# Second block: convolution taps summed in a PSUM bank, inverse roots partly in PSUM, each head's tail moved into the next head's recurrence

## The chip, the cores and the metric

The kernel is one program on one core of a Trainium2 chip. The core has five engines that matter here: TensorE (PE; its weight loads are listed as PEld), VectorE (DVE), ScalarE (ACT), GpSimd (POOL) and SyncE (SP), which issues DMAs. They share SBUF; TensorE writes into PSUM, eight banks of 512 fp32 columns on 128 partitions, which VectorE and ScalarE read and write too. The metric is the device time of one execution in microseconds, the median over several runs.

## The reference, cut to what matters

The model has two parts, one after the other, on 512 tokens of width 1024: a two-layer block, and a second block. The change lies in the first half of the second block. It computes eight heads of a gated linear recurrence (HGRN2) and a causal depthwise convolution of width 31, both from projections of the same input:

```
z = u @ w_in[l]
zq, zf, zi, zg, zca, zcb, zga, zgb = jnp.split(z, IN_SPLITS, axis=-1)
f = lb + (1.0 - lb) * jax.nn.sigmoid(zf)
o = hgrn2_chunkwise(heads(zq), heads(1.0 - f), heads(zi), heads(jnp.log(f)))
o = rms_norm_2(o, hg_norm_g[l].reshape(HG_HEADS, HG_DV)).reshape(B, S, HG_VW)
y_a = (o * jax.nn.silu(zg)) @ w_a[l]
glu = zca * jax.nn.sigmoid(zcb)
cv = causal_depthwise_conv(glu, conv_w[l], conv_b[l])
cv = jax.nn.silu(layer_norm(cv, conv_ln_g[l], conv_ln_b[l]))
y_b = cv @ w_b[l]
merged = jax.nn.sigmoid(zga) * y_a + jax.nn.sigmoid(zgb) * y_b
h = h + g1 * (merged @ w_out[l])
```

Here `hgrn2_chunkwise` is the recurrence with a decay per feature and step, and each head's output is divided by its root mean square over 128 features (`rms_norm_2`) and multiplied by a gain and by silu(zg). A layer of routed experts (PEER) follows.

## The kernel before, in words

Activations lie feature by feature: 128 features of a block on the partitions, 512 tokens along the free axis. A head of the recurrence is one such block, and so is an eighth of the convolution. Every projection unit (1024 inputs, 128 outputs) is three fp32r products, high by high, high by low and low by high, 24 matmuls of 128x512 on lines 249 to 251. Its weights come by one DMA of 512 KB; ScalarE makes the high half (line 226, `whi`), VectorE or GpSimd the low half (line 227, `wlo`).

`block2` runs a loop over eight heads. For head `hd`, `hgrn_head` is the recurrence, and a background generator is stepped 2.1 times at each of its yields: `conv_block(hd)`, which computes one eighth of the convolution, and then `hgrn_products(hd + 1)`, the four projections of the next head. What the yields set is the order in which the instructions are written down; the framework's planner then orders each engine's queue by its own estimates of when operands are ready, and the engines run these queues in that fixed order, each waiting for its operands.

`hgrn_head` goes through nine doubling levels. On a level GpSimd makes `ke` (lines 1431, 1433), VectorE makes `qe` (1435, 1437), TensorE multiplies them into a bank of the PSUM group "a" (1441 to 1466), VectorE or ScalarE copies the result out (1443 and others), and the running products `suf` (GpSimd, 1471) and `pre` (VectorE, 1472) are updated. Then TensorE forms the output in a bank of group "m", ScalarE copies it to `o` and squares it, TensorE sums the squares over the partitions (line 350), and `rsqrt` (lines 355 to 373) computes the inverse root on VectorE: a start value from the bits (362), and three Newton steps of three instructions (366 to 368), all on tiles of 128x4 in SBUF. The tail of a head follows: `rowbc` broadcasts the root to all partitions with TensorE matmuls (line 380, eight in the trace), VectorE multiplies (1491) and GpSimd multiplies by the gate (1492, `og`).

`conv_block` makes two projections and the gated input `xp`, then 31 taps. The first is ScalarE's (1325), 22 are VectorE's (1340), each adding `xp` shifted and scaled to `a`, a part of the SBUF tile `cv`; 8 are made by ScalarE (1334) and added up in `b` by GpSimd (1338). Line 1343 adds the two sums. After the loop come the projections of the two gates, `layer_stats` and `layer_norm` of the convolution, and the output products.

PSUM is cut into groups of banks by `set_banks`; block 2 runs with four banks in "m" and four in "a".

Of the kernel before, what the change touches and what calls it, by code (L numbers as in the profile page):

```python
# [11 lines left out]
I32 = mybir.dt.int32  # L12
U32 = mybir.dt.uint32
AF = mybir.ActivationFunctionType
ALU = mybir.AluOpType
P = 128
T = 512
NEG = -1.0e38
EPS = 1e-6
# [129 lines left out]
class Ker:  # L149
# [31 lines left out]
        mk = lambda n: [pool.tile([P, 2, 256], F32, tag=f"{n}{l}", name=f"{n}{l}") for l in range(2)]  # L181
        self.kT, self.vM = mk("kT"), mk("vM")

    def set_banks(self, m, a, o=0):

        self.banks.close()
        mk = lambda n, b: self.banks.enter_context(
            self.tc.tile_pool(name=n, bufs=b, space=bass.MemoryType.PSUM, reuse_waits="tile")
        )
        self.ps = {}  # L190
        for k, n in (("o", o), ("m", m), ("a", a)):
            if n:
                self.ps[k] = mk("p" + k, n)

# [157 lines left out]
                start=(b == 0 and t == 0), stop=(b == nb - 1), skip_group_check=True,  # L352
            )

    def rsqrt(self, ps, n, scale, post=1.0):

        nc, sm = self.nc, self.small
        t = lambda s: sm.tile([P, 8], F32, tag="rs_" + s, name=self.nm("rs_" + s))
        v = t("v")
        nc.vector.tensor_scalar(v[:, :n], ps, scale, EPS, ALU.mult, ALU.add)  # L360
        y = t("y")
        nc.vector.tensor_scalar(y[:, :n].bitcast(I32), v[:, :n].bitcast(I32), -0.5, 1597463007.0, ALU.mult, ALU.add)
        for i in range(3):
            last = i == 2
            a, b, y2 = t("a"), t("b"), t("y")
            nc.vector.tensor_tensor(a[:, :n], y[:, :n], y[:, :n], op=ALU.mult)  # L366
            nc.vector.scalar_tensor_tensor(b[:, :n], a[:, :n], -0.5, v[:, :n], ALU.mult, ALU.mult)  # L367
            nc.vector.scalar_tensor_tensor(y2[:, :n], b[:, :n], 1.5, y[:, :n], ALU.add, ALU.mult)
            y = y2
        if post != 1.0:  # L370
            y2 = t("y")
            nc.vector.tensor_scalar(y2[:, :n], y[:, :n], post, None, ALU.mult)
            y = y2
        return y
# [838 lines left out]
class KerC(KerB):  # L1213
# [13 lines left out]
    def block2(self, after, want):  # L1227
        nc, tc = self.nc, self.tc
        u, win = self.h, self.I["win"]
        with tc.tile_pool(name="b2", bufs=1, reuse_waits="tile") as pool:  # L1230
            og = pool.tile([P, 8, T], F32, tag="og", name="og")
            cv = pool.tile([P, 8, T], F32, tag="cv", name="cv")
            csum = pool.tile([P, T], F32, tag="csum", name="csum")
            with tc.tile_pool(name="b2h", bufs=1, reuse_waits="tile") as hp:
                bufs = {"keep": 2, "kq": KQ, "p": CP, "s": SS, "o": 3, "o1": 1, "o2": 1, "suf": 1, "b": 1}

                def f(name, tag):
                    b = bufs.get(tag, 2)
                    return hp.tile([P, T], F32, tag=tag, name=self.nm(name), bufs=b)

                sc = [hp.tile([P, 4, P], F32, tag=f"sc{i}", name=f"sc{i}") for i in range(2)]
                for s in sc:
                    nc.gpsimd.memset(s, 0.0)

                def background(hd, out):
                    yield from self.conv_block(hd, u, f, hp, cv)
                    if hd == 0:
                        nc.scalar.activation(csum, cv[:, 0, :], AF.Copy)
                    else:
                        nc.gpsimd.tensor_tensor(csum, csum, cv[:, hd, :], op=ALU.add)  # L1250
                    if hd < 7:
                        yield from self.hgrn_products(hd + 1, u, f, out)

                ins = {}
                for _ in self.hgrn_products(0, u, f, ins):
                    pass
                for hd in range(8):
                    nxt = {}
                    bg, due = background(hd, nxt), 0.0
                    for _ in self.hgrn_head(hd, f, sc[hd % 2], og, **ins):  # L1260
                        due += NC
                        while due >= 1:
                            due -= 1
                            next(bg, None)
                    for _ in bg:
                        pass
                    ins = nxt
            with tc.tile_pool(name="b2g", bufs=1, reuse_waits="tile") as gp:
                ga = gp.tile([P, 8, T], F32, tag="ga", name="ga")
                gb = gp.tile([P, 8, T], F32, tag="gb", name="gb")  # L1270
                self.gemm([win[48 + i] for i in range(8)], u, lambda i, ps, s: nc.scalar.activation(ga[:, i, :], ps, AF.Sigmoid))
                a = self.act_pair(gp, "oga", tag="p2")
                for k in range(8):
                    self.split(og[:, k, :], a[0][:, k, :], a[1][:, k, :], nc.gpsimd if k % 2 else nc.vector)
                rb = self.layer_stats(cv, csum)
                self.gemm([win[56 + i] for i in range(8)], u, lambda i, ps, s: nc.scalar.activation(gb[:, i, :], ps, AF.Sigmoid))
                b = self.new_h()
                self.layer_norm(cv, rb, b)

                def ev_a(i, ps, s):  # L1280
                    nc.vector.tensor_tensor(ga[:, i, :], ga[:, i, :], ps, op=ALU.mult)

                self.gemm([self.I["wa2"][i] for i in range(8)], a, ev_a)
                m = self.act_pair(gp, "mg", tag="p2")

                turn = {"t": 0, "q": 0, "acc": 0}

                def h2(kind):
                    i = turn[kind] = (turn[kind] + 1) % 8
                    if kind == "acc":  # L1290
                        return csum[:, i % 2 * 256 : i % 2 * 256 + 256]
                    return cv[:, i, :256] if kind == "t" else cv[:, i, 256:]

                self.h2 = h2

                def ev_b(i, ps, s):
                    nc.vector.tensor_tensor(gb[:, i, s], gb[:, i, s], ps[:, s], op=ALU.mult)
                    nc.gpsimd.tensor_tensor(ga[:, i, s], ga[:, i, s], gb[:, i, s], op=ALU.add)
                    self.split(ga[:, i, s], m[0][:, i, s], m[1][:, i, s])

                self.gemm([self.I["wb2"][i] for i in range(8)], b, ev_b, tail=3, mid=lambda hf: iter(()))

                def ev_o(i, ps, s):
                    x = self.xT[:, i, s]
                    nc.vector.scalar_tensor_tensor(x, ps[:, s], self.mod[:, 16 + i : 17 + i], x, ALU.mult, ALU.add)

                self.gemm(
                    [self.I["wo2"][i] for i in range(8)], m, ev_o, head=3, tail=4,
                    mid=lambda hf: after(slice(hf * 256, hf * 256 + 256)), want=want,
                )  # L1310

    def conv_block(self, i, u, f, pool, cv):

        nc = self.nc
# [6 lines left out]
        nc.scalar.activation(s, pss[1], AF.Sigmoid)  # L1321
        nc.vector.tensor_tensor(xp[:, K - 1 :], s, pss[0], op=ALU.mult)
        w = lambda j: self.v("conv2", j * 8 + i)
        a = cv[:, i, :]
        nc.scalar.activation(a, xp[:, 0:T], AF.Identity, scale=w(0), bias=self.v("conv2b", i))  # L1325
        b = None
        nd = ND
# [2 lines left out]
        while on_dve or on_act:  # L1330
            if on_act:
# [3 lines left out]
                if b is None:  # L1335
                    b = p
# [3 lines left out]
                nc.vector.scalar_tensor_tensor(a, xp[:, j : j + T], w(j), a, ALU.mult, ALU.add)  # L1340
            del on_dve[:2]
            yield
        nc.vector.tensor_tensor(a, a, b, op=ALU.add)

    def layer_stats(self, cv, csum):

# [57 lines left out]
        nc.scalar.activation(vt, pt, AF.Copy)  # L1404
        out.update(q=q, k=k, pre=pre, vt=vt, zg=zg)

    def hgrn_head(self, hd, f, scd, og, q, k, pre, vt, zg):

        nc, sm = self.nc, self.small
        C = lambda x, c: x[:, c * P : c * P + P]  # L1410
# [11 lines left out]
        for l in range(9):  # L1422
            m = 1 << l
# [14 lines left out]
            if m <= 16:  # L1438
                ps = self.psum()
# [4 lines left out]
            elif m == 32:  # L1444
                ps = self.psum()
# [7 lines left out]
            elif m == 64:  # L1453
                ps = self.psum()
# [3 lines left out]
            elif m == 128:  # L1458
                ps = self.psum()
# [3 lines left out]
            else:  # L1463
                ps = self.psum()
# [16 lines left out]
        o = f("o", "o")  # L1481
# [2 lines left out]
        nc.scalar.activation(sq, o, AF.Square)  # L1484
        pst = self.psum()
        self.colsum(pst, sq, 0, 1, 4)
        r = self.rsqrt(pst[:, :4], 4, 1.0 / P)
        yield
        rb = self.rowbc(r)
        t = f("t", "o")  # L1490
        nc.vector.scalar_tensor_tensor(t, o, self.v("hgn", hd), rb, ALU.mult, ALU.mult)
        nc.gpsimd.tensor_tensor(og[:, hd, :], t, zg, op=ALU.mult)

# [453 lines left out]
```

## Time and profile before

| | |
|---|---|
| median of 3 runs | 3586.81 us (3584.31 to 3593.23) |
| profiled execution | 3589.47 us |
| its span, first to last instruction | 3587.6 us |
| mean granted TensorE clock | 0.973 |
| busy: PE, DVE, ACT, POOL | 3407.2, 2391.1, 1436.3, 1313.2 us |
| head loop of the second block | about 1590 to 2050 us of the span |

A row of the profile names the line of the kernel, the engine, the operation, output and inputs (`cv<-xp,vec,cv`), shapes and a count, then busy time and the mean duration of one in ns. "Idle before" is the time that the engine stood still just ahead of these instructions, with what ended it. Times within the span are microseconds from its start. PEclk is the TensorE clock that was granted, as a share of full speed.

### The profile page before, as it was taken

How to read it: one execution, taken by the hardware profiler on the slowest of the kernel's cores; microseconds unless marked ns; L12 is line 12 of the kernel's file. 1: busy time of each engine (PE TensorE's matmuls, PEld its weight loads, DVE VectorE, ACT ScalarE, POOL GpSimd, SP SyncE). 2: the span in 40 equal slices, each digit the busy share in tenths (PEclk: the TensorE clock that was granted, in tenths of full speed). 3: DMA queues.
4: the chain of work that ended last, by engine and by line, in shares of the span. 5: the costliest groups of instructions: out<-in, count | busy, mean ns of one | idle time of the engine just before them, and what ended most of it. 6: DMA issues, size and time to landing. Idle time of an engine off the chain costs nothing.

```text
span 3587.6 us, 51001 instructions
## 1 busy us (share of the span) xinstructions
PE 3407.2 (95%) x19199; PEld 3065.0 (85%) x19199; DVE 2391.1 (67%) x4361; ACT 1436.3 (40%) x2496; POOL 1313.2 (37%) x974
## 2 busy tenths in 40 slices
PE   7999989999999999988888899998999999999999
PEld 6888788888777888876767678898999999999999
DVE  6675475445665754469898844589576654988874
ACT  4444432224555322233323332333767653333332
POOL 1322230003332210136656522246776767333310
PEclk9999999999999999998989999999999999999998
DMA  3210144221111532211111122226999898999972
GB/s 124 71 36 30 59 158 159 96 92 60 42 47 36 200 135 95 94 54 54 59 53 54 63 85 83 88 102 211 322 319 319 312 335 294 401 363 362 362 286 77
DMA packets 207350, 555.47 MB, mean 155 GB/s; under 512 B 18048, under 2 KB 85760, under 8 KB 203904
## 3 DMA queue, kind: packets, MB, share of 16 engines
q1 hardware_dynamic: 170240, 417.98, 33.3%
q0 software_dynamic: 36864, 134.23, 10.3%
q8 instruction: 151, 2.47, 0.3%
q14 instruction: 95, 0.78, 0.1%
HBM read 504.43 MB, written 47.71 MB: 154 GB/s over the span
## 4 chain that ended last, share of the span: by engine, by line
PE 54%; DVE 11%; POOL 2%; issue 2%; ACT 1%; DMA 0%; DVEq 0%; POOLq 0%; ACTq 0%
PE psa L1855 15%; PE psm L249 11%; PE psm L251 11%; PE psm L250 11%; DVE cv L1340 3%; PE psa L1800 2%; DVE wlo L227 1%; PE psa L350 1%; PE psa L380 1%; DVE rs_b L367 1%; POOL ke L1431 0%; DVE rs_a L366 0%; POOL suf L1471 0%; DVE eq L1746 0%; PE psa L1671 0%
## 5 line engine op out<-in xcount | busy, mean ns | idle before, releaser
L226 ACT ACTIVATE whi<-raw 128x1024 fp32r<-128x1024 f32 x559 | 590.9, 1059 | 1380.3 <-PE psm L250 763.7
L249 PE MATMUL psm<-hh,whi 128*128 128x512 f32 (+2 forms) x2768 | 1026.1, 371 | 25.9 <-ACT whi L226 14.8
L251 PE MATMUL psm<-hh,wlo 128*128 128x512 f32 (+2 forms) x2768 | 1007.0, 364 | 6.1 <-POOL wlo L227 4.6
L250 PE MATMUL psm<-hl,whi 128*128 128x512 f32 (+2 forms) x2768 | 1005.2, 363 | 1.3 <-DVE hl L1223 1.3
L227 DVE TENSOR_TENSOR wlo<-raw,whi 128x1024 fp32r<-128x1024 f32 x397 | 545.8, 1376 | 227.6 <-ACT whi L226 225.4
L249 PEld LDWEIGHTS psm<-hh,whi 128*128 128x128 f32 x2768 | 533.4, 193 | 81.5 <-ACT whi L226 16.1
L251 PEld LDWEIGHTS psm<-hh,wlo 128*128 128x128 f32 x2768 | 533.6, 193 | 64.4 <-POOL wlo L227 5.6
L250 PEld LDWEIGHTS psm<-hl,whi 128*128 128x128 f32 x2768 | 533.8, 193 | 52.7 <-issue 2.4
L227 POOL TENSOR_TENSOR wlo<-raw,whi 128x1024 fp32r<-128x1024 f32 x162 | 392.2, 2425 | 287.5 <-ACT whi L226 226.1
L1855 PE MATMUL psa<-gah,wlo 128*128 128x384 f32 (+2 forms) x1048 | 350.8, 335 | 0.0
L1855 PE MATMUL psa<-gah,whi 128*128 128x384 f32 (+2 forms) x1048 | 350.7, 335 | 0.0
L1855 PE MATMUL psa<-gal,whi 128*128 128x384 f32 (+2 forms) x1048 | 350.5, 334 | 0.0
L565 POOL TENSOR_TENSOR relu<-relu 128x512 f32<-128x512 f32 (+1 forms) x70 | 80.6, 1153 | 539.9 <-ACT whi L226 406.2
L1594 POOL DMA_INDIRECT rg<-in_vr_dram,rei x128 | 164.7, 1286 | 282.9 <-DVE racc L1613 267.3
L1855 PEld LDWEIGHTS psa<-gah,wlo 128*128 128x128 f32 x1048 | 200.0, 191 | 0.2 <-DVE wlo L227 0.2
L1855 PEld LDWEIGHTS psa<-gah,whi 128*128 128x128 f32 x1048 | 200.0, 191 | 0.0
L1855 PEld LDWEIGHTS psa<-gal,whi 128*128 128x128 f32 x1048 | 200.0, 191 | 0.0
L1605 DVE SCALAR_TENSOR_TENSOR rg<-rg,hT 128x1024 f32<-128x1024 f32 x128 | 153.5, 1213 | 58.5 <-DMA rg<-in_ur_dram,rei 58.4
L1340 DVE SCALAR_TENSOR_TENSOR cv<-xp,vec,cv 128x512 f32<-128x512 f32 x176 | 176.2, 1001 | 9.7 <-ACT cv L1325 7.1
L1613 DVE SCALAR_TENSOR_TENSOR racc<-rg,rw,racc 128x1024 f32<-128x1024 f32 x127 | 162.6, 1281 | 2.1 <-DMA rg<-in_vr_dram,rei 1.7
L1594 POOL DMA_INDIRECT rg<-in_ur_dram,rei x128 | 128.9, 1007 | 79.0 <-DVE rg L1605 59.7
L1772 DVE TENSOR_TENSOR oA<-io,tr 128x512 f32<-128x512 f32 x96 | 66.0, 688 | 129.2 <-PE psa L1800 115.0
(519 smaller groups left out, 6070.7 us busy)
## 6 DMA issues: line engine op xcount, KB each, us to landing
raw<-in_pu_dram SPq DMA_DIRECT2D x128, 512.0 KB, 4.8
raw<-in_pv_dram SPq DMA_DIRECT2D x128, 512.0 KB, 5.7
raw<-in_wup_dram SPq DMA_DIRECT2D x64, 512.0 KB, 3.5
raw<-in_wdn_dram SPq DMA_DIRECT2D x64, 512.0 KB, 3.5
raw<-in_win_dram SPq DMA_DIRECT2D x64, 512.0 KB, 3.4
araw<-in_ada_dram SPq DMA_DIRECT2D x48, 512.0 KB, 4.3
G<-gb SPq DMA_DIRECT2D x24, 1024.0 KB, 6.6
gt<-G SPq DMA_DIRECT2D x64, 384.0 KB, 7.9
```

Of the source, the lines that this page charges most:

```text
L226: nc.scalar.activation(hi, src, AF.Copy)
L227: (eng or nc.vector).tensor_tensor(lo, src, hi.bitcast(F32), op=ALU.subtract)
L249: nc.tensor.matmul(ps, wh[:, k, :], ah[:, kk, s], start=start, stop=False)
L250: nc.tensor.matmul(ps, wh[:, k, :], al[:, kk, s], start=False, stop=False)
L251: nc.tensor.matmul(ps, wl[:, k, :], ah[:, kk, s], start=False, stop=stop)
L565: nc.gpsimd.tensor_tensor(r, r, r, op=ALU.mult)
L1340: nc.vector.scalar_tensor_tensor(a, xp[:, j : j + T], w(j), a, ALU.mult, ALU.add)
L1594: pin(nc.gpsimd.indirect_dma_start(out=g, out_offset=None, in_=self.I["ur" if i < P else "vr"], in_offset=bass.IndirectOffsetOnAxis(ap=ei[ ...
L1605: pin(nc.vector.scalar_tensor_tensor(g, g, 1.0, hT, ALU.mult, ALU.mult, accum_out=dots[:, c : c + 1]))
L1613: pin(nc.vector.scalar_tensor_tensor(acc, g, w[:, c : c + 1], acc, ALU.mult, ALU.add))
L1800: nc.tensor.matmul(pg[:, i * P : i * P + P], A[:, i, :], B[:, i, :], start=True, stop=True)
L1855: mm = lambda o, x, y, **kw: nc.tensor.matmul(o, x, y, skip_group_check=True, **kw)
```

## The change

Three things. The VectorE taps and ScalarE's first tap are summed in a PSUM bank of a new group "c", and only the last addition writes `cv`; for the head loop the banks are cut as four "m", three "a" and one "c", and after the loop as before. `rsqrt` gets an optional room in PSUM, which the recurrence gives it in the bank of its column sums: the start value then reads a second copy of the variance from there, and the two temporaries of each Newton step lie there; `v` and `y` stay in SBUF. The tail of a head becomes a generator of its own, which is stepped after the fifth yield of the next head's recurrence (the last one after the loop).

```diff
-    def set_banks(self, m, a, o=0):
+    def set_banks(self, m, a, o=0, c=0):
...
-        for k, n in (("o", o), ("m", m), ("a", a)):
+        for k, n in (("o", o), ("c", c), ("m", m), ("a", a)):
...
-    def rsqrt(self, ps, n, scale, post=1.0):
+    def rsqrt(self, ps, n, scale, post=1.0, room=None):
...
         nc.vector.tensor_scalar(v[:, :n], ps, scale, EPS, ALU.mult, ALU.add)
+        bits = v
+        if room is not None:
+            bits = room[:, :8]
+            nc.vector.tensor_scalar(bits[:, :n], ps, scale, EPS, ALU.mult, ALU.add)
         y = t("y")
-        nc.vector.tensor_scalar(y[:, :n].bitcast(I32), v[:, :n].bitcast(I32), -0.5, 1597463007.0, ALU.mult, ALU.add)
-        for i in range(3):
-            last = i == 2
-            a, b, y2 = t("a"), t("b"), t("y")
+        nc.vector.tensor_scalar(y[:, :n].bitcast(I32), bits[:, :n].bitcast(I32), -0.5, 1597463007.0, ALU.mult, ALU.add)
+        for _ in range(3):
+            a, b = (t("a"), t("b")) if room is None else (room[:, 8:16], room[:, 16:24])
+            y2 = t("y")
...
     def block2(self, after, want):
...
+        self.set_banks(4, 3, c=1)
...
-                ins = {}
+                ins, end = {}, iter(())
...
-                    bg, due = background(hd, nxt), 0.0
-                    for _ in self.hgrn_head(hd, f, sc[hd % 2], og, **ins):
+                    bg, due, tail = background(hd, nxt), 0.0, []
+                    for n, _ in enumerate(self.hgrn_head(hd, f, sc[hd % 2], og, tail, **ins)):
+                        if n == 4:
+                            next(end, None)
...
-                    ins = nxt
+                    ins, end = nxt, tail[0]
+                next(end, None)
+            self.set_banks(4, 4)
...
     def conv_block(self, i, u, f, pool, cv):
-        a = cv[:, i, :]
+        a = self.psum("c")
...
-        nc.vector.tensor_tensor(a, a, b, op=ALU.add)
+        nc.vector.tensor_tensor(cv[:, i, :], a, b, op=ALU.add)
...
     def hgrn_head(self, hd, f, scd, og, tail, q, k, pre, vt, zg):
-        r = self.rsqrt(pst[:, :4], 4, 1.0 / P)
+        r = self.rsqrt(pst[:, :4], 4, 1.0 / P, room=pst[:, 64:88])
+
+        def end():
+            rb = self.rowbc(r)
+            t = f("t", "o")
+            nc.vector.scalar_tensor_tensor(t, o, self.v("hgn", hd), rb, ALU.mult, ALU.mult)
+            nc.gpsimd.tensor_tensor(og[:, hd, :], t, zg, op=ALU.mult)
+            yield
+
+        tail.append(end())
         yield
-        rb = self.rowbc(r)
-        t = f("t", "o")
-        nc.vector.scalar_tensor_tensor(t, o, self.v("hgn", hd), rb, ALU.mult, ALU.mult)
-        nc.gpsimd.tensor_tensor(og[:, hd, :], t, zg, op=ALU.mult)
```

## Rows read from the trace of the kernel before

**Rows 1.** Busy time by head period of the loop; all engines, then the sum.

```profile
core 0: us, PE busy (x) PEld busy (x) DVE busy (x) ACT busy (x) POOL busy (x), PEclk, DMA share, GB/s
...
1985.28:2039.16 53.88, 47.60 (x247) 39.59 (x247) 48.87 (x68) 16.83 (x26) 29.94 (x23) 0.94 0.18 59
sum 397.28, PE 338.42 PEld 280.91 DVE 360.95 ACT 124.32 POOL 241.55; mean PE 48.35 PEld 40.13 DVE 51.56 ACT 17.76 POOL 34.51
```

**Rows 2.** Waits inside the head loop: waiter, releaser, us in total, times, longest.

```profile
PE psa L380 <- DVE rs_y L368: 62.6, 8, 8.2
...
DVE pre L1472 <- POOL suf L1471: 14.7, 27, 0.6
...
DVE wlo L227 <- ACT whi L226: 8.0, 14, 2.7
DVE cv L1340 <- ACT cv L1325: 7.1, 8, 0.9
...
DVE t L1491 <- PE psa L380: 5.1, 8, 0.7
```

**Rows 3.** Timeline of TensorE around one broadcast: start, us, instruction, idle before.

```profile
1918.95 0.39 PE L250 MATMUL psm<-hl,whi 128*128 128x512 f32 x1
1927.59 2.04 PE L380 MATMUL psa<-con,rs_y 128*128 128x128 f32 x8 [8.25 <-DVE rs_y L368]
```

**Rows 4.** Busy time just after the broadcast of another head, columns as rows 1.

```profile
1870.19:1875.76 5.57, 5.57 (x17) 4.76 (x18) 4.94 (x7) 0.00 (x0) 2.56 (x2) 0.51 0.26 94
```

**Rows 5.** Instructions by line and form, head loop: busy us, mean ns, idle before.

```profile
L1340 DVE SCALAR_TENSOR_TENSOR cv<-xp,vec,cv 128x512 f32<-128x512 f32 x176 | 176.2, 1001 | 9.7 <-ACT cv L1325 7.1
...
L1338 POOL TENSOR_TENSOR b<-b,p 128x512 f32<-128x512 f32 x56 | 89.2, 1592 | 36.5 <-ACT p L1334 32.7
...
L367 DVE SCALAR_TENSOR_TENSOR rs_b<-rs_a,rs_v 128x4 f32<-128x4 f32 x24 | 15.9, 661 | 0.0
...
L366 DVE TENSOR_TENSOR rs_a<-rs_y 128x4 f32<-128x4 f32 x24 | 11.1, 462 | 0.0
L362 DVE TENSOR_SCALAR rs_y<-rs_v 128x4 int32<-128x4 int32 x8 | 10.0, 1256 | 0.0
...
L368 DVE SCALAR_TENSOR_TENSOR rs_y<-rs_b,rs_y 128x4 f32<-128x4 f32 x24 | 3.6, 151 | 0.0
```

**Rows 6.** Single lines: duration ns min/median/max, first and last start, forms.

```profile
L1340 DVE SCALAR_TENSOR_TENSOR cv<-xp,vec,cv x176: 736/752/1676, 1618.3 to 2047.2; 128x512 f32<-128x512 f32 x176
L1325 ACT ACTIVATE cv<-xp,vec x8: 812/813/815, 1617.4 to 2017.5; 128x512 f32<-128x512 f32 x8
L1343 DVE TENSOR_TENSOR cv<-cv,b x8: 691/691/695, 1652.9 to 2048.0; 128x512 f32<-128x512 f32 x8
...
L1491 DVE SCALAR_TENSOR_TENSOR t<-o,vec,psa x8: 746/746/748, 1644.0 to 2041.2; 128x512 f32<-128x512 f32 x8
...
L1746 DVE TENSOR_TENSOR eq<-eq,ixf x16: 1198/1225/3389, 2418.7 to 2805.9; 128x1024 f32<-128x1024 f32 x16
...
L1745 DVE TENSOR_TENSOR eq<-abf,io x16: 1199/1213/1222, 2417.4 to 2804.6; 128x1024 f32<-128x1024 f32 x16
...
L1696 DVE COPY io<-con x1: 279/279/279, 2404.2 to 2404.2; 128x128 f32<-128x128 f32 x1
```

**Rows 7.** Timeline of VectorE, four taps in a row.

```profile
1878.20 3.11 DVE L1340 SCALAR_TENSOR_TENSOR cv<-xp,vec,cv 128x512 f32<-128x512 f32 x4
```

**Rows 8.** Timeline of GpSimd, old tail of a head and two recurrence operations.

```profile
1873.10 1.72 POOL L1492 TENSOR_TENSOR og<-t,zg 128x512 f32<-128x512 f32 x1 [0.47 <-DVE t L1491]
...
1890.08 1.53 POOL L1431 TENSOR_TENSOR ke<-k,suf 128x512 f32<-128x512 f32 x1
1891.68 0.98 POOL L1471 TENSOR_TENSOR suf<-suf,pre 128x256 f32<-128x256 f32 x1
```

**Rows 9.** Last head's broadcast (timeline), and a later one (chain of waits).

```profile
2039.16 2.04 PE L380 MATMUL psa<-con,rs_y 128*128 128x128 f32 x8 [5.45 <-DVE rs_y L368]
...
2072.93 0.90 PE psa L380 x8
```

More of the change, by code (lines that the diff above doesn't have):

```diff
@@ L1405, in hgrn_products, with hgrn_head @@
         out.update(q=q, k=k, pre=pre, vt=vt, zg=zg)
-    def hgrn_head(self, hd, f, scd, og, q, k, pre, vt, zg):
+    def hgrn_head(self, hd, f, scd, og, tail, q, k, pre, vt, zg):
         nc, sm = self.nc, self.small
```

## The prediction

> **What bounds the kernel now.** I first cut the span by stage. The change lies in the head loop of the second block, some 460 us of the 3587.6 us span, so I cut that loop at the row broadcast of each head (line 380), which comes once per head. [rows 1] Six periods are alike, (397.28 - 53.88) / 6 = 57.2 us each; the last is 53.9 us. In a steady period VectorE is busy (360.95 - 48.87) / 6 = 52.0 us, TensorE 48.5, GpSimd 35.3, ScalarE 18. No engine is full: two nearly full ones wait for each other.
>
> The view of waits says how. [rows 2] Nearly all of TensorE's idle time is one wait: 62.6 us in 8 waits, the row broadcast waiting for the last value of the inverse root. In the timeline [rows 3] TensorE has streamed projections until 1918.95 and then stands still for 8.25 us, although other projections are queued behind the broadcast. [...] VectorE is what it waits for, and VectorE itself waits little: (14.7 + 8.0 + 7.1 + 5.1) / 8 and two small ones, 4.5 us a head.
>
> So the question is why VectorE is so late with the root. The groups by form [rows 5] show it: a convolution tap takes 1001 ns in the mean, and the root's instructions, four columns wide, take 1256, 661 and 462 ns where their sister on line 368 takes 151. [rows 6] The taps come in two kinds, about 752 ns and 1676 ns. The long ones occur while GpSimd adds the ScalarE taps (line 1338, 1592 ns). An operation with one operand in PSUM shows no such second kind: line 1491, the same operation form and size, spans 746 to 748 ns, though it lies in the same loop. Later in the kernel, line 1746 (both operands in SBUF) reaches 3389 ns, while line 1745, the same size with one operand in PSUM, stays within 1222. I read this as VectorE and GpSimd taking turns at SBUF, with one PSUM operand as the way out.
>
> **The taps.** 22 per head. Without the second kind they cost 22 x 0.752 = 16.5 us and not 22 x 1.001 = 22.0: **5.5 us** of VectorE. What no row shows is a tap that both reads and writes its sum in PSUM. The nearest are line 1491 for reading, no dearer than SBUF, and the only VectorE write into PSUM, line 1696: 279 ns for 128 columns. At no more than line 1745's 1213 / 1024 = 1.18 ns a column, 0.13 us of that is fixed, not more than the 0.151 us of a four-column instruction in SBUF (line 368). Chained taps follow one another at 3.11 / 4 = 0.78 us [rows 7]. Bounds: 0.736 us (the shortest tap, 0.4 us a head better) to 1.0 us (no gain). I take 0.75, since the nearest row is of the same form. The first tap (ScalarE, line 1325, 0.81 us) and the closing addition (line 1343, 0.69) only change the place of one operand: at nothing, by the same rows; if each grew by a third, as a tap at 1.0 us would, 0.5 us a head.
>
> [...]
>
> **The root.** Line 362 falls from 1256 to 0.15 us as its source is in PSUM: 1.1 us. Line 367 has one operand in PSUM: 3 x (0.661 - 0.15) = 1.5 us. Line 366 still squares a value from SBUF, so its 3 x (0.462 - 0.15) = 0.9 us may stay. The second start instruction (as line 368) adds 0.15. Net **2.5 us** a head; bounds 0 (if short PSUM instructions are dearer by as much) and 3.4 (line 366 freed too).
>
> **The moved tail.** Eight broadcast matmuls, one VectorE operation (747 ns) and one GpSimd multiplication (1.72 us, [rows 8]) go behind the fifth step of the next head's recurrence; no DMA moves with them. TensorE's 8.25 us wait goes, as the root is then long done, and the slow clock with it: 5.57 us at 0.51 is 2.7 us lost (the broadcast alone takes 0.90 us at the full clock, [rows 9], against 2.04). VectorE's wait for the broadcast, 5.1 / 8 = 0.6 us, goes too. What it costs: GpSimd is the chain of the recurrence, one ke and one suf, about 2.6 us, per level [rows 8], and the 1.72 us now stand between them. Queued behind it are the next level's ke and suf, for which TensorE and VectorE wait. Between 0 (GpSimd ahead) and 1.7 us; I take half, 0.9. At the old place GpSimd was idle, so nothing comes back there.
>
> **Banks.** With three banks in the group "a" the matmul of a level needs the copy of three levels before, which VectorE does ahead of the operand this matmul waits for anyway: nothing; if it came late, one operation of this width, 0.75 us a level. At the end the group is closed and the gate projections may get the bank in which the last sum lies. Between 0 and a wait that lasts through the taps of the last head: some 30 us now (from 2017.5 to 2048.0, [rows 6]), about 23 without the second kind and with the short root, of which 8 stand there today as the wait for the root and the slow clock. So 0 to 15 us, once, and at the start of the block perhaps one wait of up to 8. I take 4 for both.
>
> **The sum.** Two limits for a steady head. TensorE: 57.2 - 8.25 - 2.7 = 46.3 us. VectorE: 57.2 - 5.5 - 2.5 - 0.6 = 48.6 us, its other waits kept. VectorE stays the later one; with 0.9 for the recurrence 49.5, a gain of 7.7 us. Seven heads: 54. The last head, whose root is hardly delayed by GpSimd, loses a wait of 5.45 us [rows 9] and the slow clock: 8, less 4 for the banks. Together 58 us. The profiled execution took 3589.5 us (span 3587.6), so 3531.5; the median of the runs is 2.7 lower: 3529, rounded to **3530**.
>
> **Rivals.**
> *TensorE's limit is reached.* If the waits of 3.9 us that I left with VectorE vanish as well, a head takes 46.3 us: 8 x 10.9 = 87, less 4, so 3504. [...] Against: nearly half of them, 14.7 of 31.4 us, lie in the recurrence, whose chain the change lengthens.
> *Another wait takes the place.* VectorE runs in a fixed order, with the low halves of the weights (line 227) and the evictions among the taps. With TensorE 11 us earlier, one of them, or GpSimd's chain, may hold it up for half of what it won; then a head gains 3 us: 24 together, 3563. The same time comes out if the taps still take turns with GpSimd (then only 2.5 + 0.6 us a head are won); the narrow spread of line 1491, which also has a column of factors from SBUF, speaks against that.
> *Slower.* The sum of the taps goes through PSUM 22 times in a chain. If reading back what was just written costs there what SBUF doesn't show, a tap is longer. The gain is gone when a tap takes 0.35 us more (7.7 / 22), that is 1.1 us. At 1.5 us a head takes 49.5 + 22 x 0.75 = 66 us: 8 x 8.8 = 70 us slower, 3657. Only the chained write is unseen; 1491 and 1696 alone show no price.
> *Bank hand-over at its worst.* 15 + 8 us instead of 4: 3549.
>
> **How the numbers follow.** Forecast with 3512 to 3552 (hand-over included): 0.58. TensorE's limit, 3495 to 3512: 0.14. Another wait or taps still taking turns, 3552 to 3577: 0.17. No change: 0.04. Slower: 0.07. A change of 0.3%, 10.8 us, is about what a measurement can tell here. So faster 0.88, same 0.05, slower 0.07. The range for 8 in 10: 3500 to 3570.
>
> **What would show it.** Right: taps all near 0.75 us; line 362 near 0.15; no wait of line 380 above 1 us; granted clock 1.0 through the loop; periods near 49.5 us. Wrong: taps above 1 us; line 227, 1431 or 1441 with a new wait of several us per head; the first gate projection waiting for the last addition. The prediction fails if a head still takes 54 us or more, or less than 46.

## The result and the profile after

The changed kernel takes 3547.66 us (median of 4 runs, 3547.26 to 3551.2), the kernel before 3589.43 us on the same chip: ratio 0.9887, 95% interval 0.987 to 0.9904. That is 41.8 us less; 57 were forecast (3586.8 to 3530). The direction, the place and, within about a microsecond, the head period came out as forecast; 23 us were lost again at the two ends of the loop.

The page after, its first lines; VectorE's busy time is 64 us less, GpSimd's 27, TensorE's 17:

```profile
span 3545.5 us, 51009 instructions
...
PE 3390.6 (96%) x19199; PEld 3052.4 (86%) x19199; DVE 2327.4 (66%) x4369; ACT 1436.3 (41%) x2496; POOL 1286.5 (36%) x974
```

The head loop, cut at the last level of each head (columns as [rows 1]): the last full period and the sum over six.

```profile
1914.57:1962.90 48.33, 46.16 (x246) 38.29 (x247) 44.14 (x70) 17.76 (x29) 31.50 (x27) 1.00 0.19 66
sum 290.29, PE 277.02 PEld 229.79 DVE 265.17 ACT 106.63 POOL 191.54; mean PE 46.17 PEld 38.30 DVE 44.19 ACT 17.77 POOL 31.92
```

A period is 290.29 / 6 = 48.4 us, against 57.2. VectorE's busy time has fallen from 52.0 to 44.2 us, GpSimd's from 35.3 to 31.9, and the granted clock is 1.00 in each of the six periods, where the six before had 0.91 to 0.92 and the 5.6 us from one broadcast on 0.51 [rows 4]. Groups by form in the loop, to be set against [rows 5]; taps (line 1340 before) are line 1350 here and write the PSUM tile `psc`; the root is lines 367 to 373:

```profile
L1350 DVE SCALAR_TENSOR_TENSOR psc<-xp,vec,psc 128x512 f32<-128x512 f32 x176 | 132.1, 751 | 8.7 <-ACT psc L1335 6.9
...
L1348 POOL TENSOR_TENSOR b<-b,p 128x512 f32<-128x512 f32 x56 | 74.0, 1321 | 33.1 <-ACT p L1344 29.3
...
L371 DVE TENSOR_TENSOR psa<-rs_y 128x4 f32<-128x4 f32 x24 | 8.9, 370 | 0.0
...
L372 DVE SCALAR_TENSOR_TENSOR psa<-psa,rs_v 128x4 f32<-128x4 f32 x24 | 3.8, 159 | 0.0
...
L373 DVE SCALAR_TENSOR_TENSOR rs_y<-psa,rs_y 128x4 f32<-128x4 f32 x24 | 3.6, 150 | 0.0
...
L367 DVE TENSOR_SCALAR rs_y<-psa 128x4 int32<-128x4 int32 x8 | 1.2, 154 | 0.0
```

The single line of the taps, for [rows 6]: minimum, median and maximum are now one kind.

```profile
L1350 DVE SCALAR_TENSOR_TENSOR psc<-xp,vec,psc x176: 736/756/759, 1627.6 to 1984.7; 128x512 f32<-128x512 f32 x176
```

The taps take 751 ns in the mean and at most 759, where 1676 stood. GpSimd's additions beside them take 1321 ns and not 1592: both sides of the turn-taking are freed. The start value of the root went from 1256 to 154 ns, line 372 from 661 to 159. Line 371, whose two sources stay in SBUF, still pays (370 ns).

The start and end of every record tell which GpSimd instruction a tap ran beside. Before, 49 of the 176 taps take 1647 to 1676 ns, 48 of them beside an addition of line 1338 and one beside line 1492; the other 127 take 736 to 754 ns, 745 in the median. After, more than 80 taps run beside an addition, and none is longer than 759 ns.

TensorE's waits from the end of the norm ahead of the loop to the loop's exit, for [rows 2]:

```profile
PE psa L385 <- DVE rs_y L373: 18.5, 3, 9.1
PE psa L1476 <- DVE qe L1447: 7.7, 8, 1.1
PE psa L1457 <- DVE qe L1447: 5.0, 8, 0.7
...
PE psm L249 <- DVE cv L1353: 3.2, 1, 3.2
```

The wait of the broadcast (line 385) was about 8 us a head. Now 9.1 us of it stand at the last head and the rest ahead of the loop; within the seven periods it is gone. TensorE's waits for `qe` in the recurrence have grown instead, some 9 us in all.

**Where 23 us went.** Three rows cut the stretch in both kernels: the last `hl` of the norm before the block (its last start), the last level of the recurrence (first start in head 0, last in head 7), and the column sums of the convolution (first start). Before:

```profile
L1223 DVE SCALAR_TENSOR_TENSOR hl<-h,mod,hh x16: 471/476/1442, 1550.4 to 1579.7; 128x256 fp32r<-128x256 f32 x16
...
L1466 PE MATMUL psa<-qe,ke x32: 379/379/454, 1615.7 to 2016.1; 128*128 128x256 f32 x32
...
L350 PE MATMUL psa<-con,csum x16: 164/301/372, 2071.4 to 2086.9; 128*128 128x1 f32 x16
```

After:

```profile
L1228 DVE SCALAR_TENSOR_TENSOR hl<-h,mod,hh x16: 473/479/1347, 1547.8 to 1578.6; 128x256 fp32r<-128x256 f32 x16
...
L1476 PE MATMUL psa<-qe,ke x32: 379/379/455, 1625.1 to 1963.6; 128*128 128x256 f32 x32
...
L350 PE MATMUL psa<-con,csum x16: 164/302/373, 2031.3 to 2046.8; 128*128 128x1 f32 x16
```

| us | before | after | difference |
|---|---|---|---|
| norm's end to last level of head 0 | 1579.7 to 1615.7: 36.0 | 1578.6 to 1625.1: 46.5 | +10.5 |
| head 0 to head 7 | 400.4 (7 x 57.2) | 338.5 (7 x 48.4) | -61.9 |
| head 7 to the column sums | 2016.1 to 2071.4: 55.3 | 1963.6 to 2031.3: 67.7 | +12.4 |

So the loop's body gained 62 us, and its entry and exit gave 23 back. The timeline of TensorE at the entry, after the change (only what starts after a wait, up to the end of the norm's broadcasts):

```profile
1551.37 0.61 PE L350 MATMUL psa<-con,h 128*128 128x1 f32 x4 [1.75 <-ACT h L497]
1558.99 1.20 PE L385 MATMUL psa<-con,rs_y 128*128 128x128 f32 x4 [7.01 <-DVE rs_y L373]
1561.93 6.99 PE L350 MATMUL psa<-con,h 128*128 128x1 f32 x32 [1.75 <-ACT h L418]
1571.23 1.19 PE L385 MATMUL psa<-con,rs_y 128*128 128x128 f32 x4 [2.31 <-DVE rs_y L373]
```

Before, TensorE worked through the first half of head 0's projections in this gap (96 matmuls on the first 256 tokens, from 1552.06 on), at the full clock. The 20 us from 1550 to 1570, before:

```profile
1550.00:1570.00 20.00, 18.64 (x153) 18.22 (x153) 14.66 (x40) 9.03 (x19) 6.90 (x8) 1.00 0.24 81
```

and after:

```profile
1550.00:1570.00 20.00, 8.79 (x40) 8.35 (x40) 14.20 (x43) 6.91 (x15) 6.21 (x8) 0.56 0.16 53
```

Now it runs them from 1572.07 on, most of them after the norm: busy time between the norm's end and head 0's last level, before

```profile
1579.70:1615.70 36.00, 29.16 (x185) 23.74 (x184) 25.48 (x34) 11.51 (x17) 20.19 (x18) 1.00 0.21 74
```

and after, 270 matmuls where there were 185:

```profile
1578.60:1625.10 46.50, 41.29 (x270) 35.87 (x268) 24.81 (x34) 11.62 (x18) 19.78 (x18) 0.93 0.17 57
```

At the exit, TensorE after the last output, and the VectorE instruction that it waits for in the last row, the final addition of the convolution, which frees bank "c":

```profile
1970.07 1.86 PE L350 MATMUL psa<-con,sq 128*128 128x1 f32 x8 [3.86 <-ACT sq L1494]
1981.07 2.05 PE L385 MATMUL psa<-con,rs_y 128*128 128x128 f32 x8 [9.13 <-DVE rs_y L373]
1986.28 0.80 PE L249 MATMUL psm<-hh,whi 128*128 128x512 f32 x1 [3.16 <-DVE cv L1353]
```

```profile
1985.53 0.69 DVE L1353 TENSOR_TENSOR cv<-psc,b 128x512 f32<-128x512 f32 x1
```

The eight projections of the first gate, 24 matmuls each, start only there, 23 us after the last level. The kernel before started them 2 us after its last level (2016.1), and had run about a third of them by its last broadcast, while VectorE was at its taps:

```profile
2018.33 0.58 PE L249 MATMUL psm<-hh,whi 128*128 128x512 f32 x1
```

### The profile page after: what moved, and what is told of

It reads as the page before. It is cut to its first block, busy times and chain, and to the rows that moved or that the text cites. A ratio compares the mean times of both kernels' runs of the same rounds, so it can differ in the third digit from the quotient of the medians.

```text
span 3545.5 us, 51009 instructions
## 1 busy us (share of the span) xinstructions
PE 3390.6 (96%) x19199; PEld 3052.4 (86%) x19199; DVE 2327.4 (66%) x4369; ACT 1436.3 (41%) x2496; POOL 1286.5 (36%) x974
## 4 chain that ended last, share of the span: by engine, by line
PE 53%; DVE 10%; issue 2%; POOL 2%; DMA 1%; ACT 1%; SPq 0%; DVEq 0%; POOLq 0%; ACTq 0%
PE psa L1870 15%; PE psm L249 11%; PE psm L251 11%; PE psm L250 11%; PE psa L1815 2%; DVE psc L1350 2%; DVE wlo L227 2%; PE psa L350 1%; DVE qe L1445 1%; SPq L1838 0%; DVE pre L1482 0%; POOL wlo L227 0%; DMA raw<-in_pv_dram 0%; PE psa L1686 0%; DVE sc L1453 0%
## 5 line engine op out<-in xcount | busy, mean ns | idle before, releaser
L1350 DVE SCALAR_TENSOR_TENSOR psc<-xp,vec,psc 128x512 f32<-128x512 f32 x176 | 132.1, 751 | 8.7 <-ACT psc L1335 6.9
```

## The experiments

Times are medians against the kernel before on the same chip, with the ratio's 95% interval. Single runs of a kernel scatter by 10 us and more (13 of the kernel before, 3584.2 to 3600.1 us), so the head period and the two distances of the table above are read from each profile as well.

**1. Bank hand-over.** `c_last`, one word moved, so that "m" keeps banks 0 to 3 before, in and after the loop:

```diff
-        for k, n in (("o", o), ("c", c), ("m", m), ("a", a)):
+        for k, n in (("o", o), ("m", m), ("a", a), ("c", c)):
```

> The changed kernel with one word moved: the new bank group c is laid out behind m and a, so that m keeps the four banks it had in the stage before and in the stage after. Theory (bank hand-over): the changed kernel loses about 9 us at the entry of the loop and 12 us at its exit, because a unit of m must wait for a bank that another group still holds; with c last both go, the output of head 0 comes some 9 us earlier, the gate projections start right behind the last output, and the time is 3525 to 3531 us. Rival (the entry and exit are late for another reason, the planner's order or the last root's wait): no more than 5 us change, 3543 to 3550.

3531.63 us, ratio 0.983 (0.9808 to 0.9851). The same three rows:

```profile
L1228 DVE SCALAR_TENSOR_TENSOR hl<-h,mod,hh x16: 470/476/1325, 1558.5 to 1587.5; 128x256 fp32r<-128x256 f32 x16
...
L1476 PE MATMUL psa<-qe,ke x32: 379/379/455, 1623.6 to 1962.0; 128*128 128x256 f32 x32
...
L350 PE MATMUL psa<-con,csum x16: 164/301/370, 2016.7 to 2032.1; 128*128 128x1 f32 x16
```

Entry 36.1 us and exit 54.7, as before the change, the period 48.3 as after it. The theory holds for all 23 us: 10.4 come back at the entry and 13.0 at the exit. The exit is hardly better than before, though TensorE no longer waits for the last broadcast: one gate unit now waits for the bank of the last output, at the cost of the clock behind it (0.84 over the next 22 us).

```profile
1967.30 0.50 PE L249 MATMUL psm<-hh,whi 128*128 128x512 f32 x1 [2.73 <-ACT o L1492]
```

**2. The changed kernel again**, beside experiments 6 to 8.

> The changed kernel once more, beside the partial versions on one chip. Expected 3545 to 3552: some 62 us gained in the seven full head periods, and 10 us at the entry and 12 us at the exit of the loop lost again to the hand-over of banks.

3554.14 us, ratio 0.99 (0.9878 to 0.9921), a little above what was expected; its profile has the same distances (46.4 at the entry, 48.4 a head, 67.7 at the exit). Its interval lies above that of `c_last`: the version with "c" last beats both kernels.

**3. Only the taps.** Group "c" last; root and tail put back:

```diff
-        r = self.rsqrt(pst[:, :4], 4, 1.0 / P, room=pst[:, 64:88])
+        r = self.rsqrt(pst[:, :4], 4, 1.0 / P)
...
-        tail.append(end())
+        tail.append(iter(()))
         yield
+        rb = self.rowbc(r)
+        t = f("t", "o")
+        nc.vector.scalar_tensor_tensor(t, o, self.v("hgn", hd), rb, ALU.mult, ALU.mult)
+        nc.gpsimd.tensor_tensor(og[:, hd, :], t, zg, op=ALU.mult)
```

> Of the three parts only the taps summed in PSUM (bank group c laid out last); root and tail as before. Theory (VectorE sets the period, TensorE waits for it): the taps fall to 0.75 us, a head period from 57.2 to about 51.7 us, TensorE still waits for the root, but 2 to 3 us instead of 8; about 44 us faster than before, 3545. Rival (the wait at the broadcast sets the period and only moving the tail removes it): the period stays at 55 us or more, 3572 to 3590.

3541.59 us, ratio 0.9853 (0.9824 to 0.9882); 51.0 us a head, 6.2 less than before, of which the shorter taps make 5.5. How the rest divides was not separated: GpSimd's additions are shorter too. The broadcast still stands in its old place, and TensorE waits for it for 2 us and not 8:

```profile
PE psa L385 <- DVE rs_y L373: 15.6, 7, 2.8
```

**4. Only the tail moved.** `room`, bank "c" and both `set_banks` calls of the loop taken out, `a = cv[:, i, :]` again.

> Of the three parts only the tail of a head moved into the next head's recurrence; taps and root in SBUF, banks as before. Theory (VectorE sets the period): TensorE's wait at the broadcast goes, but TensorE then waits elsewhere for VectorE, in the recurrence; a head period stays at 56 to 57 us, 3580 to 3592. Rival (the wait and the slow clock behind it were the loss): 8 to 11 us less per head, 3500 to 3525.

3588.42 us, ratio 0.9984 (0.9965 to 1.0003), no difference that the times can tell; 56.2 us a head, 1.0 less. The view of waits shows what became of the 62.6 us: the wait moved with the tail's removal to the next instruction that needs VectorE, the recurrence's multiplication.

```profile
PE psa L1449 <- DVE qe L1443: 53.2, 9, 7.8
...
PE psa L385 <- DVE rs_y L373: 5.0, 1, 5.0
```

**5. Contention itself**, in the kernel before. This kernel leaves 7 of the 31 taps out of the sum, and with them 89.2 us of GpSimd's work [rows 5]:

```diff
-                    nc.gpsimd.tensor_tensor(b, b, p, op=ALU.add)
+                    pass
```

> The kernel before without GpSimd's additions of the ScalarE taps (7 of the 31 taps are left out of the sum). Theory (VectorE and GpSimd take turns at SBUF): the taps, still in SBUF, lose their second kind at 1676 ns, all of them near 0.75 us, and the period falls by about 5.5 us a head, 3543 to 3550. Rival (long taps come from something else, such as ScalarE reading the same input or the chain itself): the long taps stay, 3580 or more.

3540.04 us, ratio 0.9846 (0.9814 to 0.9878); 50.9 us a head. With the taps still in SBUF:

```profile
L1340 DVE SCALAR_TENSOR_TENSOR cv<-xp,vec,cv 128x512 f32<-128x512 f32 x176 | 141.1, 802 | 10.1 <-ACT cv L1325 7.5
...
L362 DVE TENSOR_SCALAR rs_y<-rs_v 128x4 int32<-128x4 int32 x9 | 1.5, 162 | 0.0
```

The taps' mean falls from 1001 to 802 ns, and the root's start value to 162 ns without any PSUM. Thirteen taps stay above 900 ns (longest 1825), and each of them runs beside another GpSimd instruction, 7 beside `ke` (line 1431) and 6 beside the tail's multiplication (line 1492). One of them, for example, starts at 1748.68 and takes 1.82 us; GpSimd's `ke` starts at 1748.70.

So the long kind comes from GpSimd, mostly from its additions, as the theory has it. The durations show this; the period does not by itself, since GpSimd's own work is shorter here too.

**6. Taps and root**, the tail at its old place (the edit of 3 without its first hunk).

> Taps in PSUM (bank group c laid out last) and the root partly in PSUM, the tail of a head at its old place. Theory (VectorE's pace sets the period, and TensorE's wait for the root is only where it shows): the root saves VectorE 2 to 2.5 us of the 51.0 us period that the taps alone gave, so 48.5 to 49 us, and moving the tail on top of that is worth less than 1 us a head; 3527 to 3537. Rival (the wait at the broadcast stays as long as the tail is in its old place): period 50.5 us or more, 3540 to 3548.

3531.19 us, ratio 0.9842 (0.9808 to 0.9876); 48.7 us a head. The wait for the root is nearly gone with the broadcast in its old place:

```profile
PE psa L385 <- DVE rs_y L373: 4.1, 6, 0.7
```

**7. Taps and tail**, the root in SBUF (only the first hunk of 3).

> Taps in PSUM (bank group c laid out last) and the tail moved, the root in SBUF as before. Theory (VectorE's pace): the tail alone gave 1.1 us a head, so 49.5 to 50.5 us a head, between the taps alone (51.0) and all three parts (48.3); 3534 to 3546. Rival (with the tail moved nobody waits for the root, so its length costs nothing): 48.3 us as with all three parts, 3525 to 3532.

3537.25 us, ratio 0.9847 (0.9825 to 0.987); 49.7 us a head, between the taps alone and all three. The root in SBUF costs 1.4 us a head (49.7 against 48.3 in experiment 1) though nobody waits at the broadcast in the loop. That it does so by keeping VectorE from other work is a reading, not shown apart.

**8. Root and tail**, the taps in SBUF.

> The root partly in PSUM and the tail moved, the taps in SBUF as before, banks as before. Theory (VectorE's pace; the taps are two thirds of its gain): 56.2 us a head with the tail alone, less 2 to 2.5 us, 53.7 to 54.2; 3565 to 3573. Rival (the taps matter only because they delay the root): a period of 50 us or less, 3540 or less.

3576.7 us, ratio 0.9967 (0.995 to 0.9985); 55.7 us a head, 1.5 us above the theory's bound, though the rival is far off.

```profile
L1348 DVE SCALAR_TENSOR_TENSOR cv<-xp,vec,cv 128x512 f32<-128x512 f32 x176 | 197.6, 1123 | 8.9 <-ACT cv L1333 7.1
...
L372 DVE SCALAR_TENSOR_TENSOR psa<-psa,rs_v 128x4 f32<-128x4 f32 x24 | 3.8, 159 | 0.0
```

The taps with the tail alone (experiment 4):

```profile
L1348 DVE SCALAR_TENSOR_TENSOR cv<-xp,vec,cv 128x512 f32<-128x512 f32 x176 | 180.3, 1025 | 9.7 <-ACT cv L1333 7.1
```

The root is short (159 ns), but the taps' mean is 1123 ns and not 1025: 22 x 0.098 = 2.2 us a head more, which takes back most of what the root saved. The records show why. With the tail alone, all eight start values of the root ran beside one of GpSimd's additions, and 56 taps were above 900 ns, 48 of them beside an addition. With the root in PSUM the start values are short, and 78 taps are above 900 ns: 56 beside an addition, 14 beside `suf`, 7 beside `qk` (line 1422) and one beside the tail's multiplication. Here the start values left the turn-taking, and taps met the additions in their place.

**9. More projections between the levels**, on `c_last`: `NC=2.4` for `NC=2.1`.

> The changed kernel with group c laid out last, and 2.4 steps of the background at each yield in place of 2.1, so that more projections stand between two levels of the recurrence on TensorE. Theory (TensorE now sets the period: 46.3 us of work and some 2 us of short waits for qe in the recurrence): with more work between the levels these waits shrink, 47.0 to 48.0 us a head, 3520 to 3530. Rival (VectorE still sets the period, and TensorE's waits only show it): 48.3 us or more, 3529 to 3540.

3539.57 us, ratio 0.9858 (0.984 to 0.9876); 49.1 us a head. The theory fell: the waits for `qe` did not shrink (18.9 us in all, against 17.0 for `c_last`), and the period grew by 0.8 us. That suits the rival; which engine the new order holds up was not shown.

**10. The tail later**, on `c_last`: `if n == 7:`.

> The changed kernel with group c laid out last, and the tail of a head taken up after the eighth step of the next recurrence in place of the fifth. Theory (the tail's place costs next to nothing, since GpSimd's multiplication fits into its idle time): 48.1 to 48.6 us a head, 3527 to 3535. Rival (the tail stands in GpSimd's chain of the recurrence and lengthens it): the place changes the period by 0.7 us or more.

3529.47 us, ratio 0.9841 (0.9822 to 0.9861); 47.9 us a head, 0.5 less than at the fifth step, between what the two expected. The times cannot tell, as the interval overlaps that of `c_last`; the period, which repeats within 0.1 us in two executions of the changed kernel, says that the fifth step costs something. That GpSimd's chain is what it lengthens was not shown.

## Why the prediction was right, and where a size was off

- *What bounds the loop.* Right. VectorE's pace sets the period. With the tail alone, the wait that the view showed moved and 1.0 us a head was won; with the taps alone, and the broadcast left in its place, 6.2 us. The largest wait in the view was the place where VectorE's lateness showed, not its cause. This holds for the 57.2 us; what sets the 48.4 that are left, with VectorE busy 44.2 and TensorE 46.2, was not taken apart.
- *The taps.* Right: 751 ns against 0.75 taken, 5.5 us a head. The unseen chained write into PSUM costs at most 11 ns a tap: 756 ns median in PSUM, 745 before for the short kind in SBUF. With the sum in PSUM all 176 taps took 736 to 759 ns, beside GpSimd's additions too. A single input in SBUF did not spare every instruction: line 362 before has one, and all eight ran beside an addition and took 1256 ns in the mean (162 without the additions, experiment 5); what sets it apart no run shows. Line 371, with two inputs in SBUF, is long in 15 of 24 cases, each beside a GpSimd instruction, and keeps its 370 ns.
- *The root.* Right. Its four lines took (15.9 + 11.1 + 10.0 + 3.6) / 8 = 5.1 us a head and take (8.9 + 3.8 + 3.6 + 1.2) / 8 = 2.2; with the added copy of the variance, 0.15, the net is 2.7, against 2.5. The period gains less: 2.3 us with the taps in PSUM and the tail at its old place (51.0 to 48.7), 1.4 with the tail moved (49.7 to 48.3), and 0.5 with the taps in SBUF (56.2 to 55.7).
- *VectorE's limit*, 48.6 us, with 0.9 for the recurrence 49.5. Measured 48.4, within 0.2 us of the limit alone. That closeness is in part luck: experiment 10 wins 0.5 us by the tail's place, so some of the 0.9 may have been there, and the limit then lies at 47.9 or below. VectorE's busy time fell by 7.8 us a head where 8.0 were forecast, its idle time by 1.0 where 0.6 was. TensorE's waits for `qe` grew by about 1.1 us a head. Its own floor, 46.3 forecast, shows as 46.2 us busy.
- *The last head.* Wrong in size: 8 us were booked for the wait and the slow clock. With the banks right, the exit gains 0.6 us (55.3 to 54.7): another wait and the slow clock took its place. In the changed kernel itself the broadcast of the last head waits 9.1 us, against the sign "no wait of line 380 above 1 us".
- *The banks.* This is the term that was mis-sized most. "I take 4 for both": against experiment 1 the runs show 10.4 us at the entry and 13.0 at the exit, 23.4 together. The exit lies within its bound of 15, the entry above its bound of 8. At the exit the mechanism was the one named, a gate unit that gets the bank of the last sum; the first gate projection waiting for the last addition was one of the signs of being wrong, and it came. At the entry it was no wait but an order: 85 matmuls that had filled TensorE's gap during the norm were queued behind it. Experiment 1 gives both back.

The sum then closes. Forecast 54 + 8 - 4 = 58; measured 61.9 + 0.6 - 23.4 = 39.1, and by the table 61.9 - 10.5 - 12.4 = 39.0. The spans differ by 42.1 us, and of the rest 1.1 lie ahead of the norm's end and 2.0 behind the column sums. The time came out where the rival "Bank hand-over at its worst" put it (3549, with 23 us for the banks), at the exit by that mechanism. That it fits within 2 us is luck: the heads won 8 us more than forecast, the last head 7 us less, and the two cancel.

## What to carry to other kernels

Look at the minimum, median and maximum of one line: two kinds of one instruction (taps of 736 to 754 and of 1647 to 1676 ns) were the sign here that VectorE and GpSimd held each other up, and with the sum of the taps in a PSUM bank both sides were freed (taps 1001 to 751 ns in the mean, additions 1592 to 1321). Before moving the instruction that waits longest, ask what the awaited engine is late with; moving the waiter alone moved the wait and won 1.0 us a head, where all three parts won 8.8. The bank borrowed for the loop was paid for at its two ends, 10.4 and 13.0 us, because the other groups shifted: lay the borrowed group out last, so that the groups that work across the border keep their banks.

## What had not been expected of the hardware

Executions reach the same point of the program at rather different times: the norm ahead of the block, whose code is the same in all of them, ended between 1572.1 us (`root_tail`) and 1592.0 us (`no_pool_adds`) of the span. Six head periods of one execution agree far better than that (48.33 to 48.41 us after the change), so a small change in one stage is read from distances within it. And what VectorE gained at one instruction it lost in part at others, beside GpSimd: with the root in PSUM and the taps in SBUF, the eight additions that the root's start values had met each met a tap instead (48 taps beside an addition, then 56), and the taps' mean rose from 1025 to 1123 ns.
